# Gathering an expert's rows with the one-hot matrix as weights, followed by a transpose and a split

## The chip, the cores and the metric

The kernel runs on one core of one Trainium2 chip. The metric is the device time of one execution in microseconds (us). TensorE (PE) does matrix products, VectorE (DVE) and ScalarE (ACT) elementwise work, GpSimd (POOL) small things, and SyncE (SP) issues the large DMA transfers. Each engine takes its instructions in the order in which the built program has them, and waits on semaphores for the others.

## The reference

Two transformer blocks follow each other on 256 tokens of width 1024. The change lies in the last layer of the second block, a mixture of experts: each token goes to two of eight experts, and each expert is a gated network with 3584 hidden channels.

```python
def moe_swiglu(x, w_router, w1, w3, w2):
    bn, s, d = x.shape                       # 1, 256, 1024
    t = x.reshape(bn * s, d)
    logits = (t @ w_router).astype(jnp.float32)
    top_val, top_idx = lax.top_k(logits, TOP_K)          # 2 of 8
    top_w = jax.nn.softmax(top_val, axis=-1)
    combine = jnp.sum(jax.nn.one_hot(top_idx, N_EXPERTS, dtype=jnp.float32) * top_w[..., None], axis=1)
    out = jnp.zeros_like(t)
    for e in range(N_EXPERTS):
        out = out + combine[:, e:e + 1].astype(t.dtype) * swiglu_2(t, w1[e], w3[e], w2[e])
    return out.reshape(bn, s, d)

def swiglu_2(x, w1, w3, w2):
    return (jax.nn.silu(x @ w1) * (x @ w3)) @ w2
```

All inputs are 32-bit floats.

## The kernel before

Every product of two 32-bit operands is made of three products of a type that TensorE takes faster (fp32r): an operand is split into a high part (ACT rounds it, line 301 for weights) and a low part (DVE subtracts, line 302), and `mm3` (line 314) multiplies high by high, low by high and high by low.

The expert stage (`moe`, from about 1636 us to the end) holds the 256 normalised token rows as two tiles by parts, `thi` and `tlo` (`hhi` and `hlo` in the code, 128 tokens x 2 x 1024). For each expert `gather` (line 1500) picks up to 128 of them. DVE writes the one-hot matrix `oh` (line 1504). Then 32 matmuls (line 1512) have a 128x128 block of `thi` or `tlo` as weights and 128 columns of `oh` moving, and give the picked rows with channels on partitions, which is the form in which `up` (line 1522) needs them. ACT and DVE by turns copy the sums out of PSUM into `xe`, two copies for the high part and two for the low (line 1514 calls `copy_alt`, so the copies have lines 787 and 789). Two transposes of `oh` and one copy (lines 1518 and 1519) give `ohT`, which puts the results back.

An expert is seven iterations of 512 hidden channels. Iteration n (0 to 55 over all experts, j = 0 to 6 in one) has these parts on TensorE, in the order in which `experts` (line 1567) writes them:

- `up` with w1: 24 matmuls of 512 columns into `p`;
- the four transposes of the previous iteration's `g` (`turn`, line 1531, which calls `transpose4`, line 553), then a split of them into `gTh` (ACT, line 319) and `gTl` (DVE, line 320);
- `up` with w3: 24 matmuls; ACT makes silu of the first sum and DVE multiplies by the second: the product `g` (lines 1584 and 1585);
- in iteration j = 6, the gather for the next expert;
- `down` of the previous iteration (line 1538): 24 matmuls into `A`, with `gTh` and `gTl`.

In j = 0 DVE and ACT also scale the last expert's result (`gated`, line 1547: two `sp` and two `gate` operations on DVE, two `sp` on ACT), and in j = 1 `scatter` (line 1557) adds it to the tokens: eight matmuls and four DVE operations on `X`.

All weights stream from memory through `chunk` (line 273): SP issues a transfer of 1 MB, ACT and DVE split it in two pieces of 128x1024, and the pieces go into tiles `h` and `lo`, of which there are three each (six pieces). Twelve pieces are one iteration: eight for `up`, four for `down`. TensorE uses a piece in six matmuls.

The order on each engine isn't written by hand. The layer in which the kernel is written puts the instructions of each engine into a fixed order when the program is built, and may move one ahead of others that are written before it, where the data allow. So the transposes of `g` can stand in the middle of an iteration's `up` part or at its start, and an ACT or DVE operation can stand several pieces earlier or later.

Of the kernel before, what the change touches and what calls it, by code (L numbers as in the profile page):

```python
# [8 lines left out]
FT = mybir.dt.float32  # L9
FR = mybir.dt.float32r  # L10
# [61 lines left out]
class Kernel:  # L72
# [1356 lines left out]
    def moe(self):  # L1429
        nc = self.nc  # L1430
        gate = self.mod(1, 1, 5)
        w1, w3, w2 = self.i_moe_w1_2[0], self.i_moe_w3_2[0], self.i_moe_w2_2[0]
        wk = self.pool("moe", 1)

        nc.gpsimd.memset(wk.tile([128, 3 * LINE], FT, name="shift"), 0.0)
        with ExitStack() as ctx:
# [6 lines left out]
            hhi, hlo = [self.hh.tile([128, 2, D], FR, name="t" + n, tag="h" + n) for n in ("hi", "lo")]  # L1443
# [6 lines left out]
            for t in range(2):  # L1450
                ts = slice(t * 128, t * 128 + 128)
                XN.append(self.norm_rows(self.mod(1, 1, 4), self.mod(1, 1, 3), t))
                for q in range(2):
                    p = self.transpose4(XN[t][:, q * 512:q * 512 + 512])
                    self.copy_alt(hf[:, 4 * q:4 * q + 4, ts], p.rearrange("p (k n) -> p k n", k=4))
                p = self.ps.tile([128, 512], FT, name="p")
# [3 lines left out]
            p = self.ps.tile([128, 512], FT, name="p")  # L1460
# [6 lines left out]
        keep, wk = wk, self.pool("moe2", 1)  # L1467
# [23 lines left out]
        p = self.ps.tile([128, 512], FT, name="p")  # L1491
# [8 lines left out]
        def gather(slot):  # L1500
            oh = wk.tile([128, 2, 128], FR, name="oh")
            ohT = wk.tile([128, 2, 128], FR, name="ohT", bufs=2)
            for t in range(2):
                nc.vector.tensor_scalar(oh[:, t], self.C["iota"], slot(t), None, op0=OP.is_equal)
            xe = []
            for n, src in enumerate((hhi, hlo)):
                x = wk.tile([128, 8, 128], FR, name=f"xe{n}")
                for q in range(2):
                    p = self.ps.tile([128, 512], FT, name="p")
                    for k in range(4):  # L1510
                        for t in range(2):
                            nc.tensor.matmul(p[:, k * 128:k * 128 + 128], src[:, t, (4 * q + k) * 128:(4 * q + k) * 128 + 128],
                                             oh[:, t], start=t == 0, stop=t == 1)
                    self.copy_alt(x[:, 4 * q:4 * q + 4], p.rearrange("p (k n) -> p k n", k=4))
                xe.append(x)
            p = self.ps.tile([128, 512], FT, name="p")
            for t in range(2):
                nc.tensor.transpose(p[:, t * 128:t * 128 + 128], oh[:, t].bitcast(FT), self.ident)
            nc.vector.tensor_copy(ohT, p[:, :256].rearrange("p (t n) -> p t n", t=2))
            return xe, ohT  # L1520
# [46 lines left out]
        def experts(jobs, first):  # L1567

            got = gather(jobs[0][3])
            prev = late = None  # L1570
            for i, (w1, w3, w2, slot, weight) in enumerate(jobs):
                w1, w3, w2 = self.wview(w1), self.wview(w3), self.wview(w2)
                xe, ohT = got
                Y = self.accs(2)
                for j in range(NB):
                    self.parts = 4 if first and i + j == 0 else 2
                    pa = up(w1, xe, j)
                    if prev:
                        gT = turn(prev[0])
                    pb = up(w3, xe, j)  # L1580
                    if j == NB - 1 and i + 1 < len(jobs):
                        got = gather(jobs[i + 1][3])
                    g = wk.tile([128, 512], FT, name="g")
                    nc.scalar.activation(g, pa, AF.Silu)
                    nc.vector.tensor_mul(g, g, pb)
                    if prev:
                        down(prev[1], prev[2], gT, prev[3])
                    if late and j == 0:
                        late = (gated(late[0]),) + late[1:]
                    if late and j == 1:  # L1590
                        scatter(*late)
                        late = None
                    prev = (g, Y, w2, j)
                if i + 1 < len(jobs):
                    late = (Y, ohT, weight)
# [9 lines left out]
        p = self.ps.tile([128, 512], FT, name="p")  # L1605
# [11 lines left out]
        row = self.norm_gain(half[0], self.i_final_norm_g_2)  # L1617
        n = nc.values_load(mosti[0:1, 0:1], min_val=0, max_val=S)
# [86 lines left out]
```

## Time and profile before

| | us |
|---|---|
| median of 3 runs (lowest, highest) | 2661.52 (2660.74, 2664.55) |
| the profiled execution: its time, its span | 2663.27, 2661.4 |
| PE busy (share of the span) | 2555.5 (96%) |
| DVE busy | 2170.3 (82%) |
| ACT busy | 1537.0 (58%) |

The profile page gives busy times by engine, groups of instructions by line and tile, and what ended the idle time ahead of them. Matmuls overlap in the pipeline, so one of 512 columns shows about 393 ns while the next starts some 227 ns after it: spacing is read from starts. Tiles have the program's names; the tile's buffer number is left out. In the profile's lines `w` and `gate` are the raw tiles into which weights land.

### The profile page before, as it was taken

Reading aid. Unit: us, or ns where it says so; the run is one execution under the profiler, and the core shown is the slowest. Engines: PE = TensorE matmul, PEld = TensorE weight load, DVE = VectorE, ACT = ScalarE, POOL = GpSimd, SP = SyncE. Lnnn points to the kernel's source line nnn. Section 1 sums busy time; section 2 is a strip of 40 time slices with the busy share of each in tenths; the row PEclk is TensorE's granted clock in tenths of the full one; section 3 lists DMA queues with packets and bytes.
Section 4 is the critical chain, followed back from the end, with each engine's and each line's share of the span. In section 5 each row is a group of like instructions: output and inputs, shape, how many; then the busy total and the mean of one; then the engine's idle time right before and its main releaser. Section 6 shows DMA issues by size and latency. Waiting matters only on the chain. (4 is left out here: it accounts for less than half of the span.)

```text
span 2661.4 us, 38016 instructions
## 1 busy us (share of the span) xinstructions
PE 2555.5 (96%) x14939; PEld 2207.7 (83%) x14939; DVE 2170.3 (82%) x2446; ACT 1537.0 (58%) x2026; POOL 207.8 (8%) x236
## 2 busy tenths in 40 slices
PE   8999999999998999899999898999999999999997
PEld 5998789989977899887998776888888887888775
DVE  6877888587478787687886976999999898988887
ACT  3454644444446545455444545777777777777775
POOL 2001200000003100231000221000000000000000
PEclk9999999999999999989999988999999999999999
DMA  9986469769553399454895746999999999999993
GB/s 341 335 310 198 174 228 332 259 216 328 179 199 112 111 320 311 157 184 143 298 323 194 239 156 224 381 347 364 347 375 342 348 350 342 348 351 349 351 343 122
DMA packets 366633, 727.33 MB, mean 273 GB/s; under 512 B 16350, under 2 KB 165072, under 8 KB 366448
## 3 DMA queue, kind: packets, MB, share of 16 engines
q1 hardware_dynamic: 362704, 717.20, 77.0%
q0 software_dynamic: 3712, 7.63, 0.9%
q8 instruction: 119, 1.95, 0.3%
q14 instruction: 66, 0.54, 0.1%
q10 hardware_dynamic: 32, 0.01, 0.0%
HBM read 723.73 MB, written 1.05 MB: 272 GB/s over the span
## 5 line engine op out<-in xcount | busy, mean ns | idle before, releaser
L302 DVE TENSOR_TENSOR lo<-w,h 128x1024 fp32r<-128x1024 f32 (+1 forms) x1062 | 1256.6, 1219 | 254.7 <-ACT h L301 248.2
L301 ACT ACTIVATE h<-w 128x1024 fp32r<-128x1024 f32 (+1 forms) x1062 | 1058.7, 1043 | 551.6 <-PE p L316 173.7
L316 PE MATMUL p<-h,xe 128*128 128x512 f32 x1792 | 574.3, 393 | 0.5 <-DVE X L1565 0.5
L316 PE MATMUL p<-hhi,h 128*128 128x256 f32 x1992 | 571.3, 287 | 0.0
L316 PE MATMUL p<-hlo,h 128*128 128x256 f32 x1992 | 567.8, 285 | 0.0
L316 PE MATMUL p<-hhi,lo 128*128 128x256 f32 x1992 | 567.6, 285 | 0.0
L316 PEld LDWEIGHTS p<-h,xe 128*128 128x128 f32 x1792 | 337.3, 188 | 70.8 <-issue 1.7
L316 PEld LDWEIGHTS p<-hhi,h 128*128 128x128 f32 x1992 | 385.3, 193 | 6.0 <-issue 2.2
L316 PEld LDWEIGHTS p<-hlo,h 128*128 128x128 f32 x1992 | 385.4, 193 | 3.3 <-issue 0.7
L316 PEld LDWEIGHTS p<-hhi,lo 128*128 128x128 f32 x1992 | 385.4, 193 | 0.5 <-issue 0.2
L316 PE MATMUL p<-lo,xe 128*128 128x512 f32 x896 | 354.9, 396 | 3.2 <-DVE lo L302 1.7
L212 DVE SCALAR_TENSOR_TENSOR macc<-mw,cond_c,macc 128x1024 f32<-128x1024 f32 x232 | 303.7, 1309 | 29.4 <-DMA mw<-in_w_ada_dram 12.5
L316 PEld LDWEIGHTS p<-lo,xe 128*128 128x128 f32 x896 | 168.7, 188 | 45.3 <-DVE lo L302 12.5
L316 PE MATMUL A<-lo,gTh 128*128 128x512 f32 x448 | 175.9, 393 | 1.3
L316 PE MATMUL A<-h,gTl 128*128 128x512 f32 x448 | 174.6, 390 | 0.0
L316 PE MATMUL A<-h,gh 128*128 128x512 f32 x440 | 172.8, 393 | 0.0
L316 PE MATMUL A<-lo,gh 128*128 128x512 f32 x440 | 171.3, 390 | 0.0
L316 PE MATMUL A<-h,gl 128*128 128x512 f32 x440 | 170.8, 389 | 0.0
L316 PE MATMUL A<-h,gTh 128*128 128x512 f32 x448 | 166.7, 391 | 0.5 <-ACT gTh L319 0.5
L316 PEld LDWEIGHTS A<-lo,gTh 128*128 128x128 f32 x448 | 84.1, 188 | 23.2 <-DVE lo L302 6.3
L316 PEld LDWEIGHTS A<-h,gTh 128*128 128x128 f32 x448 | 84.1, 188 | 18.4 <-ACT gTh L319 0.9
L316 PEld LDWEIGHTS A<-h,gTl 128*128 128x128 f32 x448 | 84.1, 188 | 17.2
(442 smaller groups left out, 3020.0 us busy)
## 6 DMA issues: line engine op xcount, KB each, us to landing
w<-in_moe_w_dram SPq DMA_DIRECT2D x306, 1024.0 KB, 6.3
w<-in_ffn_w_dram SPq DMA_DIRECT2D x165, 1024.0 KB, 7.5
mw<-in_mod_w_dram SPq DMA_DIRECT2D x144, 512.0 KB, 5.2
mw<-in_w_ada_dram SPq DMA_DIRECT2D x96, 512.0 KB, 5.4
gate<-in_moe_w_dram SPq DMA_DIRECT2D x60, 512.0 KB, 6.2
w<-in_w_in_dram SPq DMA_DIRECT2D x24, 1024.0 KB, 5.4
w<-in_mix_in_w_dram SPq DMA_DIRECT2D x17, 1024.0 KB, 5.3
w<-in_mix_out_w_dram SPq DMA_DIRECT2D x8, 1024.0 KB, 5.5
```

The lines of the kernel that those rows point to most:

```text
L212: i = nc.vector.scalar_tensor_tensor(acc, w, self.cond[blk][:, k:k + 1], acc, op0=OP.mult, op1=OP.add)
L301: nc.scalar.activation(hv[:, xs], r, AF.Copy)
L302: nc.vector.tensor_sub(lv[:, xs], r, hv[:, xs].bitcast(FT))
L316: self.nc.tensor.matmul(out, a[l][ai], b[r][bi], start=start and n == 0, stop=stop and n == 2)
```

## The change

`gather` is written anew; nothing else in the text of the kernel changes. The one-hot matrix is now the weights, and 512 channels of `thi` or `tlo` move: for each half of the channels four matmuls (two token tiles, two parts) add high and low parts in one sum. That gives the picked rows with tokens on partitions, as 32-bit values. One half is copied to a tile `row` (of the kind `sp`) by ACT, the other by DVE; each half is turned by four transposes and split again into `xe` (ACT the high part, DVE the low).

```diff
             xe = []
-            for n, src in enumerate((hhi, hlo)):
-                x = wk.tile([128, 8, 128], FR, name=f"xe{n}")
-                for q in range(2):
-                    p = self.ps.tile([128, 512], FT, name="p")
-                    for k in range(4):
-                        for t in range(2):
-                            nc.tensor.matmul(p[:, k * 128:k * 128 + 128], src[:, t, (4 * q + k) * 128:(4 * q + k) * 128 + 128],
-                                             oh[:, t], start=t == 0, stop=t == 1)
-                    self.copy_alt(x[:, 4 * q:4 * q + 4], p.rearrange("p (k n) -> p k n", k=4))
-                xe.append(x)
+            for n in range(2):
+                xe.append(wk.tile([128, 8, 128], FR, name=f"xe{n}"))
+
+            row = self.spare()
+            for q in range(2):
+                qs = slice(q * 512, q * 512 + 512)
+                p = self.ps.tile([128, 512], FT, name="p")
+                for t in range(2):
+                    for n, src in enumerate((hhi, hlo)):
+                        nc.tensor.matmul(p, oh[:, t], src[:, t, qs], start=t + n == 0, stop=t + n == 2)
+                self.copy_alt(row[:, qs], p)
+            for q in range(2):
+                p = self.transpose4(row[:, q * 512:q * 512 + 512])
+                self.split(xe[0][:, 4 * q:4 * q + 4], xe[1][:, 4 * q:4 * q + 4], p.rearrange("p (k n) -> p k n", k=4))
```

Because the order is made when the program is built, the new text also changes it in places that the diff doesn't touch. Three places follow. Line numbers from 1512 on are larger by four in the changed kernel.

First, TensorE at the first gather, at the start of the expert stage. `oh` is the one-hot matrix, `C` the constants with the identity. Before:

```order
L1607 LDWEIGHTS onesb
L1607 MATMUL p<-sel,onesb 128x8
L1512 MATMUL p<-oh,thi 128x128 x16
L1512 MATMUL p<-oh,tlo 128x128 x16
L1518 MATMUL p<-C,oh 128x128 x2
```

After:

```order
L1515 MATMUL p<-thi,oh 128x512
L1515 MATMUL p<-tlo,oh 128x512
L1515 MATMUL p<-thi,oh 128x512
L1515 MATMUL p<-tlo,oh 128x512
L1515 MATMUL p<-thi,oh 128x512
L1515 MATMUL p<-tlo,oh 128x512
L1515 MATMUL p<-thi,oh 128x512
L1515 MATMUL p<-tlo,oh 128x512
L553 MATMUL p<-C,sp 128x128 x8
L1522 MATMUL p<-C,oh 128x128 x2
```

The 32 matmuls of 128 columns have become eight of 512 columns and eight transposes.

Second, ACT in the third expert, iterations n = 17 and 18, far from any gather. `h` are pieces of weights, `gTh` the turned product of the iteration before, `g` the silu. Before:

```order
L319 ACTIVATE gTh<-p 128x512
L1584 ACTIVATE g<-p 128x512
L301 ACTIVATE h<-w 128x1024 x9
L301 ACTIVATE h<-gate 128x1024 x2
L301 ACTIVATE h<-w 128x1024
L319 ACTIVATE gTh<-p 128x512
L1584 ACTIVATE g<-p 128x512
L301 ACTIVATE h<-w 128x1024 x12
L319 ACTIVATE gTh<-p 128x512
```

After:

```order
L319 ACTIVATE gTh<-p 128x512
L301 ACTIVATE h<-w 128x1024 x2
L1588 ACTIVATE g<-p 128x512
L301 ACTIVATE h<-w 128x1024 x8
L319 ACTIVATE gTh<-p 128x512
L301 ACTIVATE h<-w 128x1024 x4
L301 ACTIVATE h<-gate 128x1024
L1588 ACTIVATE g<-p 128x512
L301 ACTIVATE h<-gate 128x1024
L301 ACTIVATE h<-w 128x1024 x6
L319 ACTIVATE gTh<-p 128x512
```

Before, `gTh` and the silu stand together behind all twelve pieces; after, `gTh` stands two and then four pieces ahead of the silu.

Third, DVE in the fifth expert's second iteration (n = 29), in which the earlier expert's result is scattered (`X`). Before:

```order
L320 TENSOR_TENSOR gTl<-p,gTh 128x512
L302 TENSOR_TENSOR lo<-gate,h 128x1024
L302 TENSOR_TENSOR lo<-w,h 128x1024 x2
L1585 TENSOR_TENSOR g<-g,p 128x512
L302 TENSOR_TENSOR lo<-w,h 128x1024 x4
L1565 SCALAR_TENSOR_TENSOR X_96<-p,comb,X_96 128x512
L1565 SCALAR_TENSOR_TENSOR X_98<-p,comb,X_98 128x512
L1565 SCALAR_TENSOR_TENSOR X_97<-p,comb,X_97 128x512
L1565 SCALAR_TENSOR_TENSOR X_99<-p,comb,X_99 128x512
L302 TENSOR_TENSOR lo<-w,h 128x1024 x6
L320 TENSOR_TENSOR gTl<-p,gTh 128x512
```

After:

```order
L320 TENSOR_TENSOR gTl<-p,gTh 128x512
L302 TENSOR_TENSOR lo<-w,h 128x1024 x2
L302 TENSOR_TENSOR lo<-gate,h 128x1024 x2
L302 TENSOR_TENSOR lo<-w,h 128x1024 x2
L1589 TENSOR_TENSOR g<-g,p 128x512
L302 TENSOR_TENSOR lo<-w,h 128x1024 x3
L1569 SCALAR_TENSOR_TENSOR X_96<-p,comb,X_96 128x512
L1569 SCALAR_TENSOR_TENSOR X_98<-p,comb,X_98 128x512
L1569 SCALAR_TENSOR_TENSOR X_97<-p,comb,X_97 128x512
L1569 SCALAR_TENSOR_TENSOR X_99<-p,comb,X_99 128x512
L302 TENSOR_TENSOR lo<-w,h 128x1024 x3
L320 TENSOR_TENSOR gTl<-p,gTh 128x512
```

Between the product `g` and the `X` operations stand three pieces where four stood, and three pieces in place of six between `X` and `gTl`.

## Rows read from the trace of the kernel before

**Rows 1.** Windows of an early and a late expert: PE, PEld, DVE, ACT, POOL, clock, DMA, GB/s.

```profile
1869.00:1993.00 124.00, 123.83 (x577) 102.75 (x577) 114.19 (x113) 93.28 (x102) 0.00 (x0) 1.00 0.98 360
2365.00:2492.00 127.00, 125.91 (x576) 101.94 (x575) 112.92 (x112) 91.40 (x102) 0.00 (x0) 1.00 0.96 348
```

**Rows 2.** Waits, 1760 to 1885 us: who waited for whom, total, times, longest.

```profile
ACT h L301 <- PE p L316: 17.8, 27, 3.0
```

**Rows 3.** Waits, 2385 to 2510 us.

```profile
ACT gTh L319 <- PE p L553: 18.3, 6, 4.2
PEld p L316 <- DVE lo L302: 2.8, 5, 0.8
```

**Rows 4.** Timeline of PE: start, us, engine, line, operation; iterations 5 and 6.

```profile
1728.76 0.60 PE L553 MATMUL p<-C,g 128*128 128x128 f32 x4
...
1745.56 0.60 PE L553 MATMUL p<-C,g 128*128 128x128 f32 x4
...
1751.48 1.90 PE L1512 MATMUL p<-oh,thi 128*128 128x128 f32 x16
...
1755.17 0.48 PE L316 MATMUL A<-h,gTh 128*128 128x512 f32 x1
...
1766.17 0.60 PE L553 MATMUL p<-C,g 128*128 128x128 f32 x4
```

**Rows 5.** Timeline at the first gather.

```profile
1636.65 3.68 PE L1512 MATMUL p<-oh,thi 128*128 128x128 f32 x16 [0.54 <-DVE mosti L1611]
...
1643.84 0.78 PE L316 MATMUL p<-h,xe 128*128 128x512 f32 x1
```

**Rows 6.** Windows at the first gather; the granted clock is third from the end.

```profile
1640.00:1644.00 4.00, 4.00 (x21) 4.00 (x21) 0.91 (x2) 0.60 (x1) 0.00 (x0) 0.50 0.52 188
...
1646.00:1648.00 2.00, 2.00 (x9) 1.55 (x9) 0.00 (x0) 0.00 (x0) 0.00 (x0) 0.86 0.00 0
```

**Rows 7.** Groups, 1636 us to the end: copies of gathered rows; busy us, mean ns.

```profile
L789 DVE CAST xe<-p 128x512 fp32r<-128x512 f32 x16 | 10.8, 683 | 5.5 <-PE p L1512 5.5
L787 ACT ACTIVATE xe<-p 128x512 fp32r<-128x512 f32 x16 | 9.5, 592 | 13.0 <-PE p L1512 12.6
```

**Rows 8.** Timeline of PE, late experts: transposes of `g`, one late matmul.

```profile
2094.58 0.27 PE L553 MATMUL p<-C,g 128*128 128x128 f32 x1
...
2112.31 0.49 PE L553 MATMUL p<-C,g 128*128 128x128 f32 x3
...
2583.57 0.60 PE L553 MATMUL p<-C,g 128*128 128x128 f32 x4
...
2596.80 0.61 PE L316 MATMUL A<-h,gTh 128*128 128x512 f32 x2
2597.52 0.50 PE L316 MATMUL A<-lo,gTh 128*128 128x512 f32 x1
...
2601.53 0.60 PE L553 MATMUL p<-C,g 128*128 128x128 f32 x4
```

**Rows 9.** Timeline of ACT and DVE in the iteration from 2583.57 us.

```profile
2584.21 0.60 ACT L319 ACTIVATE gTh<-p 128x512 fp32r<-128x512 f32 x1 [4.05 <-PE p L553]
...
2595.64 0.69 DVE L1585 TENSOR_TENSOR g<-g,p 128x512 f32<-128x512 f32 x1 [0.65 <-PE p L316]
2596.25 5.76 DVE L302 TENSOR_TENSOR lo<-w,h 128x1024 fp32r<-128x1024 f32 x5
```

**Rows 10.** Timeline of DVE, then PE, iterations 42 and 43: gating and scatter.

```profile
2402.72 1.28 DVE L1552 TENSOR_TENSOR sp<-A,gate 128x512 f32<-128x512 f32 x2
...
2420.46 2.73 DVE L1565 SCALAR_TENSOR_TENSOR X<-p,comb,X 128x512 f32<-128x512 f32 x4 [0.66 <-PE p L1563]
2423.10 2.35 DVE L302 TENSOR_TENSOR lo<-gate,h 128x1024 fp32r<-128x1024 f32 x2
...
2419.80 0.39 PE L1563 MATMUL p<-sp,ohT 128*128 128x512 f32 x1
...
2424.57 0.27 PE L553 MATMUL p<-C,g 128*128 128x128 f32 x1
```

## The prediction

> **What bounds the kernel now.** I read the windows first, expert by expert. Only the expert stage holds gathers, so only it can change: eight gathers, eight experts. In an early expert TensorE is busy 123.83 of 124 us at granted clock 1.00, and DVE 114.19 [rows 1]. TensorE sets the pace there, and ACT waits for it to give tiles back [rows 2]. A late expert has the same work and is some 3 us longer, and in it PE is no longer busy throughout [rows 1]. The waits say why: ACT stands 18.3 us in front of `gTh`, and TensorE's own short waits are for `lo` [rows 3]. No wait names a transfer; weights are there in time.
>
> The timeline shows the two kinds of iteration. An early one, from transposes to transposes, takes 16.80 us: 72 matmuls of 512 columns and four transposes [rows 4]. One with a gather takes 20.61, so 34 instructions of 128 columns cost 3.81, 0.112 each; the 72 are left with (16.80 - 0.45)/72 = 0.227 each, and a piece of weights (six matmuls) lasts TensorE 1.36. A late one takes 17.96 [rows 8]. There ACT idles 4.05 until the transposes come, and cannot go round `gTh` to the next cast [rows 9]. DVE makes the product `g` with one piece of `lo` beyond it done: the first piece of `down` runs, the second must wait for `g` and a piece on DVE, and the matmul at 2597.52 comes 0.49 us after its forerunner has started, not 0.23 [rows 8, 9].
>
> So I take the order, not the profile, for one count: how many `lo` pieces DVE has finished at product n beyond those that `up` of iteration n needs. I call it pieces in hand. Before, it is 4 or 3 up to n = 24, then 2, 1, 2, and from n = 28 in each expert 4, 2, 2, 1, 1, 1, 1 (once 2 for the first 1). Ordinary iterations with one in hand are n = 26, 31 to 33, 39, 40, 45 to 47, 52 to 54. Read as in [rows 8] (17.73 for n = 26, 17.96 for n = 53), those twelve lose 0.68 to 1.19 each against 0.227 a matmul, 12.6 together, 1.05 on average. Iterations with two or more lose 0.15 at most, but for n = 38 with 0.7. Gather iterations in the late experts lose 0.5.
>
> **The change, part by part.** *TensorE in the gathers.* Seven gathers stand amid full-speed work: 34 instructions, 3.81, go; 8 x 0.227 + 10 x 0.112 = 2.94 come. That is 0.87 each, 6.1 in all. The first gather runs at the lower clock level (0.50, that is 1.2 GHz; the clock rises after 1646 [rows 6], some 9.4 us after TensorE began to work without a break) and takes 7.19 from its first matmul to the first `up` [rows 5]. After: eight matmuls at twice 0.213 are 3.4; ACT copies half a row in 0.59 while they run; DVE copies the other in 0.68 behind the last [rows 7]; four transposes at about 0.22 follow, the split takes a copy on each engine, two transposes of `oh` close it. That makes about 5.8, 1.4 less. As the time gained is at half speed and the clock may rise at the same moment, it is worth 0.7 to 1.4; I take 0.7. Sum of the gain: 6.8.
>
> A price from a page speaks against this part. The Trainium skill (TensorE: Matmul & The Clock Gate, section Back-to-back issue gap, and the section on 56 ns above it) gives about 55.6 ns between warm 128-column matmuls and 215.7 between those of 512. By it a gather would go from 34 x 0.056 = 1.9 to 2.3, a loss of 0.4, and seven of them would add 2.7 where I subtract 6.1; the time would be 2681. This trace has 112 and 227 ns for the two [rows 4], and the measurement decides.
>
> *ACT and DVE in the gathers.* Each gets a copy more: 0.59 and 0.68 a gather [rows 7]. In the early experts DVE has 9.8 us free in an expert [rows 1], so nothing. TensorE's transposes wait for these copies; in the order the first four stand behind all eight matmuls and the next behind three to five matmuls of `down`, which is as long as a copy. Zero, with 0 to 0.9 a gather as bounds (DVE first has to finish a piece).
>
> *The new order.* This is the larger part, and the diff doesn't show it. Counted in the same way, pieces in hand after the change are as before up to n = 12, then 3, 4, 2, 2, and from n = 17 on never above 2: one at 17 to 21, two at 22 and 23, one at 24 to 26, two at 27; then in each expert 1 (j = 0), 2, 2 and ones, with n = 38 and n = 49 also at 2. Two things differ. The poor state begins ten iterations earlier. And before, each gather let DVE refill to four, since TensorE spent 3.8 us there without using a piece; now the gather is shorter, DVE has more to do in it, and j = 0 begins with one.
>
> Priced by kind:
>
> - Five more ordinary iterations at one (n = 17, 18, 19, 24, 25): 5 x 1.05 = 5.3. One more gather iteration at one (n = 20): 0.5.
> - Four j = 0 at one (n = 21, 28, 35, 42), where DVE also does the gating. The trace has no such case; I follow it by hand. Behind the product DVE makes three pieces, two `sp` (1.20), one piece, two `gate` (1.20), three pieces, `gTl` (0.66), pieces; a piece every 1.135 [rows 9, 10]. From the end of `up`, the second piece is ready at 2.03 while TensorE is through with its first at 1.36: wait 0.67. The fifth, behind `sp`, at 6.64 against 6.11: 0.53. The sixth, behind `gate`, at 8.98 against 8.45: 0.53. Later ones are in time. That is 1.7 each, 6.8. The bounds are 0 (full hand, as before) and 2.4.
> - n = 49, gating with two in hand, followed in the same way: 0.5.
> - Five scatters with two in hand (n = 22, 29, 36, 43, 50). Before, the same case lost nothing, by a hair: TensorE enters the scatter at 2419.80, its eight matmuls end at 2421.62, the two pieces that DVE had made ahead of `X` last to 2424.35, and the next is ready at 2423.10 + 1.22 = 2424.32 [rows 10]. After, three pieces stand between product and `X`, not four, so one is left for TensorE: with it and the transposes, 2421.62 + 1.36 + 0.45 = 2423.43, and it waits 0.9. Five times: 4.5. Bounds 0 and 1.4 (a whole piece).
>
> Sum: 5.3 + 0.5 + 6.8 + 0.5 + 4.5 = 17.6 lost. SP's transfers follow the release of raw tiles by DVE; they only get later with DVE, and a slower stage asks less of memory (348 GB/s where the early expert took 360 [rows 1]). POOL's order in this stage is unchanged.
>
> **The sum.** 17.6 - 6.8 = 10.8 us more in the profiled span of 2661.4, thus 2672.2. The profiled execution took 2663.27 in all, 1.87 more than its span, and the median of the runs is 2661.52; I set the difference on the median: 2672.
>
> **The rivals.** *Waits cost only like for like*: the nine further iterations with one in hand (five ordinary, four j = 0) cost 1.05 each, the gather 0.5, and the gating and the scatters nothing, because DVE gets ahead while TensorE is in the scatter's matmuls. 10.0 - 6.8 = 3.2: 2665, no measurable difference. For it: two in hand nearly always sufficed before. Against it: the scatter had 0.03 us to spare [rows 10]. It decides at the scatter: this rival holds if PE's wait behind `X` stays under 0.2. Chance 0.22.
>
> *The order isn't the cause*: the late experts are slower for something else (the stretch, the memory), and the new order costs nothing. Then the gathers' gain stands alone: 2655, faster. Against it: in one expert, full-hand iterations take 16.8 and the others 17.96, at the same clock. Chance 0.06.
>
> *Gathers lose as well*: in the five late gathers TensorE also waits for the copies and splits, the gain of 0.87 goes and up to 0.4 is added, the first gains nothing: 5 x 1.3 + 0.7 = 7.2 more, 2679. For it: DVE enters them with one piece in hand. Chance 0.11.
>
> *Small matmuls are as cheap as the page says*: 2681, with 0.01, as its rows say otherwise.
>
> **How the numbers follow.** My forecast has 0.60. A measurement of this kernel can tell about 0.2% (5.3 us) from no change. Faster: 0.06. Within 0.2%: 0.22. Slower: 0.60 + 0.11 + 0.01 = 0.72. The lower end takes all nine iterations at 0.68, the gather at 0.5, nothing for the rest, and 7.5 of gain: 2661. The upper end takes the forecast with the gathers' loss of 7.2: 2680.
>
> **What would show it.** Right: a gather stretch of about 2.9 us; iterations of 16.8 to n = 15 and of about 17.9 from n = 17; experts from the third gather on of 128 to 130 us from gather to gather where they took 125 to 127; ACT's waits for `gTh` in the third and fourth experts, where there were next to none; a PE wait of about 0.9 behind each late scatter. Wrong: late experts no longer than before (then the count of pieces doesn't set the waits), iterations with one in hand at 16.8, or gathers with long waits of PE for `sp`.

## The result and the profile after

The changed kernel takes 2674.55 us (median; 2671.98 to 2681.22), the kernel before, beside it, 2661.13 (2655.14 to 2664.55): a ratio of 1.006, 95% interval 1.0047 to 1.0073. It is slower, by 13.4 us between the medians; the forecast was 10.8 more, 2672.

Its profiled execution took 2675.62 us with a span of 2673.8. An early expert is a little shorter than the one of [rows 1], and PE is as busy throughout; a late one (iterations 41 to 47, from transposes to transposes) is 130.3 us long where the 127 us of [rows 1] stood, and PE idles 3.7 us in it. The windows, with columns as in [rows 1]:

```profile
1738.00:1861.00 123.00, 122.80 (x560) 101.24 (x559) 114.59 (x114) 93.73 (x103) 0.00 (x0) 1.00 0.99 356
2371.50:2501.80 130.30, 126.59 (x560) 100.28 (x559) 113.67 (x113) 91.58 (x103) 0.00 (x0) 1.00 0.94 339
```

The waits in that late expert answer to [rows 3]: who waits for whom, total, times, longest.

```profile
ACT gTh L319 <- PE p L553: 25.2, 6, 4.5
PEld p L316 <- DVE lo L302: 6.5, 9, 1.6
...
PE p L316 <- DVE lo L302: 2.6, 3, 1.4
...
DVE X L1569 <- PE p L1567: 1.8, 1, 1.8
...
DVE sp L1556 <- PE A L316: 1.3, 1, 1.3
```

ACT's wait for the transposes has grown from 18.3 to 25.2, TensorE's weight loads wait 6.5 for `lo` where they waited 2.8. The last row is one that the prediction doesn't speak of: DVE's `sp`, the first step of the gating, waits 1.3 us for TensorE's `A`.

The timeline of PE at a gather amid full-speed work, iteration 6, answers to [rows 4] (start, us, engine, line, operation):

```profile
1738.22 0.60 PE L553 MATMUL p<-C,g 128*128 128x128 f32 x4
...
1744.13 0.39 PE L1515 MATMUL p<-thi,oh 128*128 128x512 f32 x1
...
1745.95 0.66 PE L553 MATMUL p<-C,sp 128*128 128x128 f32 x4
1746.36 0.47 PE L316 MATMUL A<-h,gTh 128*128 128x512 f32 x1
...
1758.06 0.60 PE L553 MATMUL p<-C,g 128*128 128x128 f32 x4
```

The iteration takes 19.84 us (1738.22 to 1758.06) where it took 20.61, so the gather costs 3.04 over the 16.80 of an ordinary one. Far from a gather, two consecutive groups of transposes in the third expert, early in the stage:

```profile
1945.62 0.60 PE L553 MATMUL p<-C,g 128*128 128x128 f32 x4
...
1963.27 0.60 PE L553 MATMUL p<-C,g 128*128 128x128 f32 x4
```

Iteration 18 takes 17.65, not 16.80. Ordinary iterations up to n = 16 have no such loss, those from 17 on do.

**The books.** From the starts of the transposes every iteration has a length; I take off 0.227 for each matmul of 512 columns and 0.112 for each of 128 that start in it [rows 4]. What remains is its loss. The stage is counted from the first gather's first matmul to the end of the span.

| us | before | after | difference | predicted |
|---|---|---|---|---|
| first gather to first transposes of `g` | 24.90 | 22.21 | -2.7 | -0.7 |
| the seven gathers' own matmuls (7 x 0.87) | | | -6.1 | -6.1 |
| loss of ordinary iterations | 13.7 | 17.0 | +3.3 | +5.3 |
| loss of the seven gather iterations | 1.7 | 4.5 | +2.8 | +0.5 |
| loss of the three iterations of each gating and scatter | 1.4 | 21.3 | +19.9 | +11.8 |
| last group of transposes to the end | 28.69 | 28.53 | -0.2 | 0 |
| the stage | 1024.8 | 1041.8 | +17.0 | +10.8 |

The two profiled executions differ by 12.4 us of span, not 17.0, because the changed one began its first gather at 1631.99 and the other at 1636.65. Up to about there both programs, and all kernels below, have the same instructions in the same order on PE, DVE and ACT (but for one matmul near 1533 us, which starts up to three places later in three, six and seven); their first gathers began between 1628.7 and 1640.4. That part of the program varies from run to run, so I compare stages and losses, each of one profiled execution: an ordinary iteration with a full hand takes 16.77 to 16.83 in all of them. The very end of the stage varies too. From the last matmul of `down` on, all kernels have nearly the same work left, and it took 18.5 to 19.0 us in seven of the traces but 16.5 in those of three, six and seven; why isn't known. A stage of one of these three is some 2 us shorter for this alone.

### The profile page after: what moved, and what is told of

It reads as the page before. It is cut to its first block, busy times and chain, and to the rows that moved or that the text cites. A ratio compares the mean times of both kernels' runs of the same rounds, so it can differ in the third digit from the quotient of the medians.

```text
span 2673.8 us, 37780 instructions
## 1 busy us (share of the span) xinstructions
PE 2552.3 (95%) x14811; PEld 2188.7 (82%) x14811; DVE 2174.8 (81%) x2454; ACT 1536.7 (57%) x2034; POOL 207.7 (8%) x236
## 5 line engine op out<-in xcount | busy, mean ns | idle before, releaser
L316 PE MATMUL p<-lo,xe 128*128 128x512 f32 x896 | 357.9, 399 | 16.5 <-DVE lo L302 13.9
L316 PE MATMUL A<-h,gTh 128*128 128x512 f32 x448 | 159.7, 392 | 0.5 <-ACT gTh L319 0.5
L319 ACT ACTIVATE gTh<-p 128x512 fp32r<-128x512 f32 x56 | 33.2, 593 | 140.6 <-PE p L553 137.1
L316 PEld LDWEIGHTS A<-h,gTh 128*128 128x128 f32 x448 | 84.1, 188 | 18.3 <-ACT gTh L319 0.9
```

The lines of the kernel that those rows point to most:

```text
L316: self.nc.tensor.matmul(out, a[l][ai], b[r][bi], start=start and n == 0, stop=stop and n == 2)
L319: self.nc.scalar.activation(hi, src, AF.Copy)
```

## The experiments

**One: every gather twice, in the old form.** It makes TensorE do more, and in the order built from it DVE has three or four pieces in hand at every product.

```diff
-                        for t in range(2):
+                        for t in (0, 1, 0, 1):
                             nc.tensor.matmul(p[:, k * 128:k * 128 + 128], src[:, t, (4 * q + k) * 128:(4 * q + k) * 128 + 128],
```

> The kernel before, with the 32 gather matmuls issued twice in every gather (same sums, more work for TensorE). In the order that comes out, DVE has 3 or 4 pieces in hand at every product, in the late experts too. Theory (the pieces in hand set the waits): TensorE's extra work costs 7 x 32 x 0.112 = 25 us and some 7 more in the first gather at half clock, and the 16.8 us of waits of the late experts go: about 15 us slower than before, 2676, and every ordinary iteration takes 16.8. Rival (the late experts are slower for something else, the order doesn't matter): the extra work is added to what was there, 32 us slower, 2693, and late iterations still take 17.9.

Measured: 2680.51 (2677.53 to 2685.66) beside 2660.00 for the kernel before, ratio 1.0069 (1.0044 to 1.0093). The twelve poor iterations are gone: all ordinary iterations together lose 0.1 us where they lost 13.7, and the seven gathers cost 24.17 - 20.59 = 3.58 more each. Waits of the late expert that answers to [rows 3]:

```profile
ACT h L301 <- PE p L316: 17.7, 27, 3.0
ACT h L301 <- PE A L316: 17.6, 15, 4.2
DVE lo L302 <- ACT h L301: 12.6, 23, 3.1
```

Neither ACT's wait for the transposes nor TensorE's for `lo` is there. Of the rival's 32 us, 13.8 came back as waits that ended; the order is worth that much. The doubled first gather adds 6.9 us at the lower clock level (31.8 to the first transposes for 24.9), as the theory had it. The theory's 2676 is 4.5 short: 3.0 of its 16.8 us of waits stay, nearly all as some 0.45 in each iteration with a scatter; the rest isn't explained.

**Two: no gathers but the first.** All experts then work on the first expert's rows, so the output isn't the reference's.

```diff
-                    if j == NB - 1 and i + 1 < len(jobs):
-                        got = gather(jobs[i + 1][3])
```

> The kernel before, with the first gather alone: experts 1 to 7 use the rows of expert 0, so the work of seven gathers is left out and the output is another. In the order that comes out, the pieces in hand are nearly those of the changed kernel (2 and 1 from the third expert on). Theory: 7 x 3.8 = 26.7 us of work go and some 24 us of waits come (excess about 41 in place of 16.8), 2658, so hardly faster than before, with waits of about 2.6 in the scatter iterations as in the changed kernel. Rival (the order doesn't matter): 26.7 us faster, 2634.

Measured: 2667.15 (2660.67 to 2673.64), ratio 1.0024 (1.0009 to 1.0039). Less work takes longer. The stage is 1030.8; 26.7 us of matmuls (seven times 3.81) are gone, and losses of 33.1 have come. The rival, by which the gathers' matmuls are simply time, falls. The theory's mechanism holds, since the waits came; its 2658, a little faster than before, was 9 us too low. Some 24 us of new waits were expected and 33.1 came, and the largest part lies around gating and scatter: 27.0 us, where the kernel before loses 1.4 and the changed kernel 21.3.

**Three and four: an order held by hand, for both kernels.** The split of the transposes, silu, and product are kept where they are written, the last two behind `down`; the gating is written in j = 1 and the scatter in j = 2, each behind `up` with w1, with their first operations kept there. This gives four pieces in hand at every product. (The helpers that carry the hold, and the old places of gating and scatter, aren't shown here.)

```diff
                     pa = up(w1, xe, j)
+                    if late and j == 1:
+                        late = (gated(late[0], True),) + late[1:]
+                    if late and j == 2:
+                        scatter(*late, True)
+                        late = None
...
-                    g = wk.tile([128, 512], FT, name="g")
-                    nc.scalar.activation(g, pa, AF.Silu)
-                    nc.vector.tensor_mul(g, g, pb)
                     if prev:
                         down(prev[1], prev[2], gT, prev[3])
+                    g = wk.tile([128, 512], FT, name="g")
+                    self.tc.keep_in_program_order(nc.scalar.activation(g, pa, AF.Silu))
+                    self.tc.keep_in_program_order(nc.vector.tensor_mul(g, g, pb))
```

The kernel before, so held:

> The kernel before with the old gather, where DVE's and ACT's split of g, silu and product, gating and scatter are held behind the pieces that are written ahead of them: 4 pieces in hand at every product. Theory: the 16.8 us of waits go, 2645 (2642 to 2650), and iterations take 16.8 throughout. Rival: no change, 2661.

Measured: 2658.36 (2651.69 to 2662.74), ratio 0.9989 (0.9975 to 1.0003). By the time alone the rival (2661, no change) looks right. The trace says otherwise: the ordinary iterations lose 0.2 us in all where they lost 13.7, but the gather iterations lose 9.1 where they lost 1.7, and those around gating and scatter 5.4 where they lost 1.4. The timeline of ACT, then PE, in iteration 27:

```profile
2115.72 0.58 ACT L1535 ACTIVATE gTh<-p 128x512 fp32r<-128x512 f32 x1
2116.53 2.01 ACT L301 ACTIVATE h<-gate 128x1024 fp32r<-128x1024 f32 x2 [0.23 <-PE p L316]
2122.83 0.60 ACT L787 ACTIVATE xe<-p 128x512 fp32r<-128x512 f32 x1 [4.29 <-PE p L1512]
```

```profile
2119.62 0.33 PE L1512 MATMUL p<-oh,thi 128*128 128x128 f32 x2
...
2122.35 1.34 PE L1512 MATMUL p<-oh,thi 128*128 128x128 f32 x11
```

The new order put ACT's first copy of gathered rows two pieces behind `gTh`. It stands 4.29 us for the gather's matmuls, most of which TensorE does behind `up`, and all later pieces stand behind it. The hold had made a wait of its own. It costs 1.5 us in iterations 27 and 41, and 3.1 in 34 and 48. In these two the granted clock fell to 0.50 for 3.4 us, from amid the gather on and after TensorE had stood waiting in it, so some 3.2 of the 9.1 are the clock's. The window in iteration 34, columns as in [rows 1]:

```profile
2251.62:2255.03 3.41, 3.41 (x14) 3.02 (x14) 3.41 (x5) 1.98 (x3) 0.00 (x0) 0.50 0.30 67
```

The changed kernel, so held:

> The changed kernel with the same hold on the order: 4 pieces in hand at every product. Theory: waits of 42.8 us go nearly all and the gather's own gain stands alone, 2637 to 2642, that is 3 to 8 us less than the kernel before with its order held (7 x 0.87, and 1 to 2.6 in the first gather). Rival (the new gather is itself dearer, by waits of TensorE for its copies): slower than the kernel before with its order held.

Measured: 2640.40 (2635.29 to 2642.82), ratio 0.9918 (0.9892 to 0.9944): faster than both kernels. Here no such copy stands in the way. Windows, columns as in [rows 1], the second over ten late iterations:

```profile
1741.00:1864.00 123.00, 122.78 (x558) 100.92 (x557) 113.62 (x113) 93.86 (x103) 0.00 (x0) 1.00 0.99 360
2325.00:2500.00 175.00, 174.96 (x799) 144.29 (x798) 156.99 (x156) 131.62 (x148) 0.00 (x0) 1.00 0.96 355
```

PE is busy 174.96 of 175 us: late experts run as early ones do, with the same weights from memory. What made them slower in both kernels was the order. All losses together are 4.4 us where the changed kernel has 42.8.

**Five and six: the change in two parts.** The old `gather` stays, the new one stands beside it as `gather_new`. First only the first gather, then only the seven others, are new.

```diff
-            got = gather(jobs[0][3])
+            got = gather_new(jobs[0][3])
```

> The kernel before, with only the first of the eight gathers written in the new way. Theory (the order, and with it the waits, is turned by the seven gathers amid full-speed work, not by the first; the first gather alone gains what the changed kernel's trace shows, 2.65 us to the first transposes): the pieces in hand read from the order are before's up to n = 19, with one more ordinary iteration at one (n = 25). So -2.65 + 1.05 = -1.6: the stage from the first gather to the end takes 1023.2 us where before's profiled run has 1024.8, the sum of excess over the spacing of full-speed matmuls is 18 (before 16.8), and the time is 2658 beside 2660. Rival 1 (the first gather gains the predicted 0.7 only): a stage of 1025.1. Rival 2 (the first gather's text already turns the order): a stage of some 1035 to 1040 and 2672 or more.

```diff
-                        got = gather(jobs[i + 1][3])
+                        got = gather_new(jobs[i + 1][3])
```

> The kernel before, with the seven later gathers written in the new way and the first left as it was. Theory: the order's pieces in hand are the changed kernel's from n = 18 on (one less poor iteration, n = 17), so the waits are its 26.0 more than before's less 0.9, the seven gathers gain 6.1 and the first nothing: a stage of 1024.8 + 25.1 - 6.1 = 1043.8, and a time of 2660 + 19 = 2679 (2676 to 2682), slower than the changed kernel by the first gather's 2.65 less 0.9. Rival (the first gather is what turns the order): 2654.

Measured: the first alone 2657.70 (2654.83 to 2661.81), ratio 0.9991 (0.9981 to 1.0000), stage 1022.8, losses 17.5; the seven alone 2678.46 (2675.02 to 2685.47), ratio 1.0079 (1.0055 to 1.0103), losses 42.2. Both are as the theory had them; the stage of the seven is 2 us under its 1043.8, and the 2 us are those of the short end. The first gather brings 2.7 us to the first transposes and leaves the order, with one more poor iteration. The gathers amid full-speed work turn it. The medians' differences, -3.9 and +16.9 (beside 2661.57), add up to 13.0, the whole change's being 13.4.

**Seven: the kernel before, held, with its gather together.** As three, and the first matmul of a gather is kept behind `up`.

```diff
-                            nc.tensor.matmul(p[:, k * 128:k * 128 + 128], src[:, t, (4 * q + k) * 128:(4 * q + k) * 128 + 128],
-                                             oh[:, t], start=t == 0, stop=t == 1)
+                            i = nc.tensor.matmul(p[:, k * 128:k * 128 + 128], src[:, t, (4 * q + k) * 128:(4 * q + k) * 128 + 128],
+                                                 oh[:, t], start=t == 0, stop=t == 1)
+                            if n + q + k + t == 0:
+                                self.tc.keep_in_program_order(i)
```

> The held order of e3_before_order_held on the kernel before, and TensorE's first matmul of each gather kept where it is written, so that a gather's 32 matmuls stand together. Theory (what e3 lost is ACT's first copy of gathered rows, which stood two pieces behind the transposes' split and waited 4.3 us for matmuls that TensorE did last, with pieces queued behind it): the gathers' 9.1 us of waits of e3 go, the scatters keep theirs (0.4 to 0.5 each and 0.4 in the iteration after, as in e3). Stage 1020.3 - 9.1 = 1011 to 1014, time 2648 to 2651. Beside e4_after_order_held (stage 1002.9), it prices the new gather alone under one order: 8 to 11 us of stage (seven times 0.8, 2.65 at the first). Rival (e3's loss comes from elsewhere, the hand of pieces does not set the time in the kernel before): 2658 again, waits unchanged.

Measured: 2645.94 (2644.85 to 2652.00), ratio 0.9947 (0.9928 to 0.9965), stage 1011.8. ACT in iteration 27, to be set beside the rows of three:

```profile
2122.82 1.07 ACT L301 ACTIVATE h<-w 128x1024 fp32r<-128x1024 f32 x1 [0.71 <-PE p L316]
2126.38 0.60 ACT L787 ACTIVATE xe<-p 128x512 fp32r<-128x512 f32 x1 [2.49 <-PE p L1512]
```

The copy stands a piece later and waits 2.49, not 4.29; TensorE waits no longer, and the gather iterations lose 0.3. So the cause of three's shortfall is shown, and the kernel before, too, gains when its order has four pieces in hand. Beside four (stage 1002.9) this prices the new gather with both orders held: 8.9 us of stage gained. Parted, the first gather brings 3.5, the seven others 6.1 and smaller losses 1.5, and 2.2 go off because the trace of seven has the short end and that of four a long one. The medians of the two kernels differ by 5.5.

**Eight: the changed kernel, held, but gating and scatter left to the build.** Four pieces in hand at every product, `sp` directly behind the product in five experts.

```diff
-                    if late and j == 1:
-                        late = (gated(late[0], True),) + late[1:]
-                    if late and j == 2:
-                        scatter(*late, True)
-                        late = None
...
+                    if late and j == 0:
+                        late = (gated(late[0]),) + late[1:]
+                    if late and j == 1:
+                        scatter(*late)
+                        late = None
```

> e4_after_order_held with the gating and the scatter back where the build puts them: four pieces in hand at every product, but in five experts the two `sp` of the gating stand directly behind the product in j = 0, ahead of the next pieces. Theory (the missed term: `sp` reads `A`, which TensorE ends only with the last matmul of `down`, 5.45 us behind the product; DVE stands idle some 4.3 us and the four pieces in hand are gone by then): TensorE waits about 1.9 for the first piece behind `sp`, 0.95 behind `gate`, and 1.2 behind the scatter, 4.05 an expert, 20 in five: 2658 to 2662. Rival (as the prediction had it, gating costs DVE only its 2.4 us of work, and four pieces in hand cover it): 2640 to 2642, as e4.

Measured: 2652.87 (2649.06 to 2660.54), ratio 0.9976 (0.9964 to 0.9988), stage 1018.6. Beside four the stage is 15.7 us longer (the median 12.5); 20 were expected, so the time lies below its 2658 to 2662, and the rival (nothing) falls. First the changed kernel's timeline, DVE, then PE, in the gating of the fourth expert's result:

```profile
2144.02 0.69 DVE L1589 TENSOR_TENSOR g<-g,p 128x512 f32<-128x512 f32 x1 [0.65 <-PE p L316]
2144.63 3.49 DVE L302 TENSOR_TENSOR lo<-w,h 128x1024 fp32r<-128x1024 f32 x3
2149.41 1.29 DVE L1556 TENSOR_TENSOR sp<-A,gate 128x512 f32<-128x512 f32 x2 [1.29 <-PE A L316]
2150.62 1.22 DVE L302 TENSOR_TENSOR lo<-w,h 128x1024 fp32r<-128x1024 f32 x1
2151.75 1.29 DVE L1558 TENSOR_TENSOR gate<-sp 128x512 fp32r<-128x512 f32 x2
```

```profile
2151.89 0.50 PE L316 MATMUL p<-lo,xe 128*128 128x512 f32 x1 [1.40 <-DVE lo L302]
2154.23 0.50 PE L316 MATMUL p<-lo,xe 128*128 128x512 f32 x1 [0.69 <-DVE lo L302]
```

And the same place in eight, with four pieces in hand:

```profile
2134.95 0.68 DVE L1601 TENSOR_TENSOR g<-g,p 128x512 f32<-128x512 f32 x1
2137.58 1.29 DVE L1564 TENSOR_TENSOR sp<-A,gate 128x512 f32<-128x512 f32 x2 [1.95 <-PE A L316]
2138.79 1.22 DVE L302 TENSOR_TENSOR lo<-w,h 128x1024 fp32r<-128x1024 f32 x1
2139.92 1.29 DVE L1566 TENSOR_TENSOR gate<-sp 128x512 fp32r<-128x512 f32 x2
```

```profile
2140.06 0.50 PE L316 MATMUL p<-lo,xe 128*128 128x512 f32 x1 [1.39 <-DVE lo L302]
2142.40 0.50 PE L316 MATMUL p<-lo,xe 128*128 128x512 f32 x1 [0.69 <-DVE lo L302]
```

The waits agree to 0.01 us. `sp` reads `A`, and `A` is complete only with the last matmul of `down`. Whatever DVE had in hand at the product, `down` has by then used, unless pieces for the next `up` stand between product and `sp`. In the changed kernel one in hand and three behind the product make the four that `down` needs (for n = 49 two and two), in eight four in hand and none behind it: nothing is left for `up`. Iterations 29, 36, 43 and 50 (and 22) lose 2.6 each in both kernels; the iterations after them lose 0.82 to 0.87 in both. In the kernel before, four in hand and three behind the product left three, and the wait was nothing. My 4.05 an expert was 0.6 too much (I had DVE idle for 4.3 us; it idled 1.95, being late with the product).

## Why the prediction was right, and where its steps failed

The forecast of slower, 2672, stands against 2674.55, and its cause against each rival. Step by step:

- *The seven gathers' matmuls.* Right. The predicted 2.94 us measured 3.04 in iteration 6, against 3.81. By the 55.6 and 215.7 ns that the prediction took from the Trainium skill (TensorE: Matmul & The Clock Gate) the new form would cost more than the old; the trace doesn't agree: a gather iteration fell from 20.61 to 19.84. The rival built on that falls. The section it names, Back-to-back issue gap, gives such figures for isolated matmuls only; for a stream with weight loads it has about 81 and 131 ns, and an estimate from these (2.75 before, 1.86 after) is a gain. The trace's spacings, 112 and 227, are neither pair.
- *The first gather.* The mechanism was right, the size not: its length fell from 7.19 to 5.75 as worked out (5.8), but I took only half, 0.7, for the case that the clock rises at the same moment. It rose earlier, and the whole was worth 2.7 (last section).
- *The count of pieces.* Right in place and kind. Poor iterations begin at n = 17; the 17 ordinary ones with one in hand lose 0.65 to 1.13, and the five further ones 4.8 together where I had 5.3. The table's row grew by only 3.3, because ordinary iterations that were poor before lost some 1.5 less. One, three, four, seven and eight show the count as the cause: with three or four in hand, ordinary iterations lose 0.1 to 0.2 in all. The rival by which the order isn't the cause (2655) falls with one and two.
- *Gather iterations.* Half right. I had 0.5 for one further at one piece in hand; the five late ones lose 4.35 together (0.53 to 1.02 each), and the sum is 2.8 more than before. With four in hand (four, eight) they lose 0.00 to 0.16 each. So the new copies cost next to nothing by themselves (TensorE's waits for `sp` come to 0.8 us in the changed kernel's whole stage), and the rival with 7.2 falls; the poor order and the gather together cost more than I took.
- *The scatter.* Right: 0.9 predicted, 0.84 to 0.87 measured in the iteration behind `X`, five times. This decides against the like-for-like rival (2665), whose condition was under 0.2. The timeline of DVE, then PE, of the changed kernel in iteration 29:

```profile
2169.76 2.73 DVE L1569 SCALAR_TENSOR_TENSOR X<-p,comb,X 128x512 f32<-128x512 f32 x4 [1.80 <-PE p L1567]
```

```profile
2173.68 0.50 PE L316 MATMUL p<-lo,xe 128*128 128x512 f32 x1 [0.56 <-DVE lo L302]
```

- *The gating.* Mis-sized, and the step that failed. I followed DVE by hand through j = 0 and let it run `sp` when it came to it, 1.7 us of loss an expert and 0.5 in the last, 7.3 in all. But `sp` waits for `A`, a wait that the sum has at nothing, though its own timeline held it: there DVE comes to `sp` at 4.30 (6.64 - 1.20 - 1.135), and TensorE ends `down` at 6.11. The stretch costs 2.64 an expert for that, 13.2, and 3.3 more in the iterations before, from the single piece in hand. Eight shows that the first part doesn't depend on the hand at all. The row that would have told it is [rows 10]: there `sp` starts with no wait, because three pieces for `up` stood ahead of it; I read that as a property of `sp`, not of what stood before it.

So the stage grew by 17.0, not by 10.8. Gating and scatter cost 8.1 more than forecast and the gather iterations 2.3; the first gather and the ordinary iterations cost 2.0 less each and hid part of that. The medians differ by 13.4. That the time came within 3 us of the forecast is thus partly luck. In the profiled pair the part ahead of the stage took 4.7 us less in the changed kernel; what it took in the other runs no profile shows.

## What to carry to other kernels

Where an order is built from the text, a local edit is priced twice: what its instructions cost, and what the new order leaves ready ahead of the engine that sets the pace. Count, at each wait of the engine that supplies it, the pieces that will still be unused when that wait ends, not when it begins; an operation that reads a finished sum waits for the last matmul of it, so put work for the next step ahead of it. When an edit that saves work is slower, hold the order and measure again before dropping it: here the same edit was worth 8.9 us of the stage (5.5 by the medians) with the order held, and the two together 0.8% of the time.

## What the hardware showed that was not expected

The clock at the start of the stage. With the old gather it stayed at 0.50 (1.2 GHz) through all its matmuls of 128 columns and rose only after `up` had begun: in the kernel before some 9.9 us after the first of them (0.86 over 1646 to 1648 puts the rise at 1646.56 [rows 5, 6]). In two, three, six and seven, which have the old first gather too, it rose 9.0 to 9.7 us after the first, again with `up` begun. With every gather doubled it stayed there for the whole of the 14 us of such matmuls and rose behind the first matmuls of 512 columns, which begin at 1654.40; the windows of that kernel, the granted clock third from the end:

```profile
1640.00:1654.00 14.00, 13.61 (x64) 13.61 (x64) 1.88 (x10) 1.44 (x4) 0.00 (x0) 0.51 0.43 157
1654.00:1657.00 3.00, 3.00 (x10) 2.52 (x10) 1.41 (x4) 0.00 (x0) 0.00 (x0) 0.50 0.00 0
1657.00:1659.00 2.00, 2.00 (x9) 1.63 (x9) 0.00 (x0) 0.19 (x1) 0.00 (x0) 0.90 0.00 0
```

With the new gather, eight matmuls of 512 columns at the start, it was at 1.00 (2.4 GHz) before `up` had run half a microsecond. The timeline of PE, then the windows, of the changed kernel:

```profile
1631.99 0.79 PE L1515 MATMUL p<-thi,oh 128*128 128x512 f32 x1 [0.53 <-DVE mosti L1615]
...
1635.57 2.10 PE L553 MATMUL p<-C,sp 128*128 128x128 f32 x8
1637.46 0.52 PE L1522 MATMUL p<-C,oh 128*128 128x128 f32 x2
1637.74 0.48 PE L316 MATMUL p<-h,xe 128*128 128x512 f32 x1
```

```profile
1636.00:1638.00 2.00, 2.00 (x10) 1.67 (x10) 1.19 (x2) 0.89 (x2) 0.00 (x0) 0.56 1.01 372
1638.00:1640.00 2.00, 2.00 (x10) 1.60 (x10) 1.41 (x4) 0.31 (x1) 0.00 (x0) 1.00 0.10 34
```

So the first 2.7 us of `up` (1643.84 to 1646.56), at the lower level in the kernel before, run at the higher one and take half: 1.3 us, which with the 1.4 of the shorter gather make the 2.7 of the books. When it rises varied among the four kernels with the new first gather, from about 3 us after its first matmul (four) to 6 (eight). Whether it is the width of the matmuls that decides, or something else in which the two gathers differ, isn't settled by these runs.
